# Samples of the cross-attention with the queries as the stationary operand, state space parameters worked out in the input projection, and part of each state space pass on GpSimd

## The chip, the cores and the metric

One core of one Trainium2 chip runs one execution of the kernel. The metric is the device time of that execution in microseconds (us), and it is compared with the time of the kernel before, on the same chip. The engines are named as in the profile: PE is TensorE's matrix multiplication and PEld its weight load, DVE is VectorE, ACT ScalarE, POOL GpSimd, and SP the SyncE queue that issues most transfers.

## What is computed

The reference is one step of a one-layer decoder trunk in float32, for a prompt of 1024 tokens and for 8 samples of 8 tokens each. What matters here:

```python
z = h @ p['w_in']                    # query latent | kv latent | rotary key | state space input
c_q, c_kv, k_r, u = z[..., :256], z[..., 256:512], z[..., 512:544], z[..., 544:]
attn_out = mla_mixer(c_q, c_kv, k_r, pos, p, past)   # samples: 8192 cached positions, paged

# state space: 32 groups of 16 channels, 64 complex states each
dt = jnp.exp(p['ssm_log_dt'])[:, None]
mag = jnp.exp(dt * a_re)
abr, abi = mag * jnp.cos(dt * a_im), mag * jnp.sin(dt * a_im)
bbr, bbi = fr * b_re - fi * b_im, fr * b_im + fi * b_re
# h[t] = a h[t-1] + b u[t], an associative scan over time
y = einsum('blgn,gcn->blgc', hr, c_re) - einsum('blgn,gcn->blgc', hi, c_im) + d * u

# cross-attention, 4 heads of 128, 256 memory tokens
s = jnp.einsum('bqhd,bmhd->bhqm', q, mk) * MEM_SCALE
o = jnp.einsum('bhqm,bmhd->bqhd', softmax(s), mv)
```

The prompt's cross-attention has keys and values of its own, made in this step; each of the 8 samples reads its keys and values (256 tokens, 4 heads) from a cache.

## The kernel before

The work stands in stages, one after the other in the span: the input projection (`stage_in`, to about 131 us), the parallel stage (`stage_par`, 131 to 699), attention over the prompt, the mix, the cross-attention (`stage_mem`, 994 to 1204) and the feed-forward part.

**Input projection.** `stage_in` walks over nine row tiles, t = 8 (the samples) first and then 0 to 7, and multiplies each with the weights of the combined projection (three matmuls per block, since float32 numbers are split into a high and a low half). At t = 2 it calls `dec_start`, which prepares the decode attention and issues its first gathers.

**Parallel stage.** `gen_dec` is the attention of the samples over their cached positions: 16 steps, each with two gathers of latent rows (`kf`) and two of rotary keys (`rf`) that GpSimd issues as indirect DMAs (L1011). `kf` has two buffers, so the gather for step n + 2 waits until step n's value matmuls (`ov`, L1109) have read the buffer. In each step DVE turns the gathered blocks (nine 128x1024 transposes, L1033), PE makes the scores `S` (L1044), DVE takes their maximum `mx` (L1065), ACT the exponentials, PE turns those (`pt`, L1093) and makes `ov`. Beside it run, one after the other, the generators `gen_ssm`, `gen_glu` and others. All instructions of both sides go through the class `Order`, a list scheduler that estimates each instruction's cost and writes the order of PE, DVE, ACT and POOL from that; each engine then runs its list in order.

**State space (`gen_ssm`).** First a parameter part (L617 to L737), some hundred small DVE operations on 128 x 32 to 128 x 256 elements: exponentials as polynomials, angles, powers `pw`, tables `cs8` and `phk` of phases; it loads `prm`, and the samples' inputs `us` in eight scattered loads (L623) that 32 small PE transposes (L736) turn to `Us`. Then eight passes of four groups each. `load(q)` brings `bc` and `h` (L759); `tables(q)` makes W1 (through W1T, transposed on PE at L806), W2 (128 x 576 in three operations, on DVE: two products, `W<-Cst,pw` and `big<-bc,pw`, and their difference `W<-W,big`) and W3, and fills the phase table `csn` by four turns, each doubling its length: two products `big<-csn,phk` and two results `csn<-big,big`. `csn` has one buffer. `chunks(q)` multiplies the inputs with W1, rotates by `csn`, scans (L868), rotates back to `H` and multiplies with W2 and W3. L889 stands for the samples in a chunk, four matmuls a pass, eight in the trace since a float32 matmul is recorded as two. Most elementwise operations go through a helper that the profile shows as L611, so they are told apart by tiles.

**Cross-attention (`stage_mem`).** The prompt goes through in eight tiles; between the tiles stands a list `sample`, pieces of the samples' attention. Before: `sample_k(b)` loads the keys of sample b, 128 x 1024, into a buffer `kv` and makes the scores in eight matmuls (L1777) with a 128 x 128 block of keys stationary and 8 columns of queries moving; `sample_w` and `sample_pT` do the softmax of all samples at once; `sample_v(b)` makes the values the same way (L1809), with a block of values stationary and 8 columns of weights moving. `kv` has two buffers.

## Time and profile before

| | us |
|---|---|
| runs | 2022.9, 2007.9, 2007.51; median 2007.9 |
| profiled execution | 2011.3 |
| its span, first to last instruction | 2009.5 |
| PE busy | 1875.4 (93%) |
| DVE busy | 1099.2 (55%) |
| ACT busy | 802.3 (40%) |
| POOL busy | 515.9 (26%) |

Shares over the whole span hide that stages have different limits, so the windows view cuts the span at the stages' ends: for each stretch its length, the busy time of each engine with its number of instructions, and the granted clock of TensorE as a share of full speed. The views by line give the mean duration of a group of equal instructions; the timeline gives single instructions with their start and duration; the chain of waits follows the work that ended last.

### The profile page before, as it was taken

What the parts mean: (1) busy time and instruction counts of PE and PEld (TensorE: products, weight loads), DVE (VectorE), ACT (ScalarE), POOL (GpSimd) and SP (SyncE); (2) the same over time, 40 slices, a digit from 0 to 9 for tenths busy, and PEclk for the clock granted to TensorE, in tenths of its full rate; (3) what the DMA queues carried; (4) which work ended last, traced back from release to release, by engine and by line L of the source; (5) the groups of instructions that cost most, each with busy time, mean ns of one, the idle gap of its engine ahead of it and who ended that gap; (6) DMA issues with size and microseconds to landing.
All of it is one profiled execution on the core that took longest, in us unless ns stands there. A gap on an engine that the chain in (4) does not pass through costs nothing.

```text
span 2009.5 us, 32068 instructions
## 1 busy us (share of the span) xinstructions
PE 1875.4 (93%) x12747; PEld 1486.4 (74%) x12747; DVE 1099.2 (55%) x2000; ACT 802.3 (40%) x1578; POOL 515.9 (26%) x549
## 2 busy tenths in 40 slices
PE   8967799789898899999999989999999999999997
PEld 6853455355454588777788978888888999999776
DVE  4238999775556588843334464443545533334333
ACT  5312233143332378853333344333444333333332
POOL 1312111131121033325301022222144421110554
PEclk9988889899899999999979999999999999999999
DMA  7713534455477511141123453223333522222221
GB/s 245 234 41 123 198 129 146 143 207 190 156 255 265 151 55 40 64 147 38 66 92 99 148 179 121 93 86 105 94 114 108 170 85 85 81 78 88 74 80 62
DMA packets 136550, 247.94 MB, mean 123 GB/s; under 512 B 26897, under 2 KB 91217, under 8 KB 132305
## 3 DMA queue, kind: packets, MB, share of 16 engines
q1 hardware_dynamic: 129072, 169.87, 27.0%
q0 software_dynamic: 7328, 76.03, 9.9%
q8 instruction: 100, 1.64, 0.3%
q14 instruction: 50, 0.40, 0.1%
HBM read 217.13 MB, written 27.29 MB: 122 GB/s over the span
## 4 chain that ended last, share of the span: by engine, by line
PE 74%; DVE 8%; DMA 6%; issue 5%; ACT 4%; POOL 1%; SPq 1%; DVEq 0%; ACTq 0%; POOLq 0%
PE ps L2069 26%; PE z L1581 5%; PE ps L335 4%; PE ps L337 4%; PE ps L336 4%; PE z L488 4%; PE S L1044 3%; PE ov L1109 3%; DVE kT L1033 2%; PE b L1736 2%; DMA kf<-in_cache_kv_dram,idx 2%; PE t L1384 1%; DMA W<-ky 1%; PE b L335 1%; PE b L336 1%
## 5 line engine op out<-in xcount | busy, mean ns | idle before, releaser
L2069 PE MATMUL ps<-xTl,wh 128*128 128x288 f32 (+1 forms) x1056 | 288.4, 327 | 0.0
L2069 PE MATMUL ps<-xTh,wh 128*128 128x288 f32 (+1 forms) x1056 | 288.2, 327 | 0.0
L2069 PE MATMUL ps<-xTh,wl 128*128 128x288 f32 (+1 forms) x1056 | 288.2, 327 | 0.0
L326 POOL TENSOR_TENSOR wl<-st,wh 128x1024 fp32r<-128x1024 f32 (+1 forms) x52 | 115.8, 2227 | 410.9 <-ACT wh L325 410.9
L1044 PE MATMUL S<-kT,Qb 32*64 32x512 f32 x2304 | 161.6, 663 | 39.2 <-DVE kT L1033 18.0
L326 DVE TENSOR_TENSOR wl<-st,wh 128x1024 fp32r<-128x1024 f32 (+1 forms) x52 | 62.1, 1195 | 246.0 <-ACT wh L325 246.0
L325 ACT ACTIVATE wh<-st 128x1024 fp32r<-128x1024 f32 (+1 forms) x104 | 102.5, 994 | 234.2 <-PE ps L2069 212.5
L2069 PEld LDWEIGHTS ps<-xTh,wh 128*128 128x128 f32 x1056 | 180.1, 189 | 14.1
L2069 PEld LDWEIGHTS ps<-xTl,wh 128*128 128x128 f32 x1056 | 180.0, 189 | 13.8
L2069 PEld LDWEIGHTS ps<-xTh,wl 128*128 128x128 f32 x1056 | 179.9, 189 | 13.9
L326 DVE TENSOR_TENSOR wdl<-std,wdh 128x1024 fp32r<-128x1024 f32 x44 | 100.3, 2282 | 147.3 <-ACT wdh L325 147.3
L1033 DVE STREAM_TRANSPOSE kT<-kf 128x1024 f32<-128x1024 f32 x128 | 151.6, 1220 | 25.2 <-DMA kf<-in_cache_kv_dram,idx 17.5
L2020 POOL TENSOR_TENSOR al<-act,ah 128x1024 fp32r<-128x1024 f32 x44 | 106.8, 2426 | 174.0 <-ACT ah L2019 174.0
L335 PE MATMUL ps<-wdh,ah 128*128 128x512 f32 x352 | 139.5, 396 | 0.0
L336 PE MATMUL ps<-wdl,ah 128*128 128x512 f32 x352 | 139.1, 395 | 0.0
L1109 PE MATMUL ov<-kf,PT 128*64 128x256 f32 x1024 | 128.7, 399 | 0.6 <-ACT PT L1094 0.6
L337 PE MATMUL ps<-wdh,al 128*128 128x512 f32 x352 | 126.1, 396 | 0.0
L1044 PEld LDWEIGHTS S<-kT,Qb 32*64 32x64 f32 x2304 | 44.2, 142 | 98.5 <-issue 41.2
L1109 PEld LDWEIGHTS ov<-kf,PT 128*64 128x64 f32 x1024 | 71.3, 142 | 52.1 <-issue 18.1
L2019 ACT ACTIVATE ah<-act 128x1024 fp32r<-128x1024 f32 (+1 forms) x44 | 49.0, 1113 | 142.2 <-PE ps L336 141.4
L335 PEld LDWEIGHTS ps<-wdh,ah 128*128 128x128 f32 x352 | 66.2, 188 | 17.4 <-issue 0.8
L337 PEld LDWEIGHTS ps<-wdh,al 128*128 128x128 f32 x352 | 66.1, 188 | 15.6
(532 smaller groups left out, 3972.9 us busy)
## 6 DMA issues: line engine op xcount, KB each, us to landing
st<-in_w_gate_dram SPq DMA_DIRECT2D x22, 1024.0 KB
st<-in_w_up_dram SPq DMA_DIRECT2D x22, 1024.0 KB
std<-in_w_down_dram SPq DMA_DIRECT2D x44, 512.0 KB
x<-in_x_prompt_dram SPq DMA_DIRECT2D x16, 512.0 KB
x<-x2d SPq DMA_DIRECT2D x15, 512.0 KB
wst<-in_w_in_dram SPq DMA_DIRECT2D x8, 528.0 KB
xT<-in_xT_dram SPq DMA_DIRECT2D x8, 512.0 KB
ws<-in_w_out_dram SPq DMA_DIRECT2D x8, 512.0 KB
```

What stands on the lines that cost most here:

```text
L325: nc.scalar.activation(hi, src, AF.Copy)
L326: (lo_eng or nc.vector).tensor_sub(lo, src, hi.bitcast(F32))
L335: mm(ps, lh, rh, start=start, stop=False)
L336: mm(ps, lh, rl, start=False, stop=False)
L337: mm(ps, ll, rh, start=False, stop=stop)
L488: nc.tensor.matmul(z[:P, :c1 - c0], lhs[:, k, :P], rhs[:, k, c0:c1], start=a, stop=b)
L1033: V.transpose(t, RF[n] if kb == 8 else KF[n][:, :, :, kb * 32:kb * 32 + 32])
L1044: nc.tensor.matmul(SS[n][half[a], j], Qb[q, kb, 2 * p + a], ts[q, a], start=kb == BLOCKS[0], stop=kb == BLOCKS[-1])
L1109: nc.tensor.matmul(ov[half[a]], PTS[n, g][:, m, half[a]], KF[n][:, a, g * 4 + m], start=g == 0 and m == 0, stop=g == 3 and m == 3)
L1581: nc.tensor.matmul(z[n], l, r[:, n * 512:(n + 1) * 512], start=a, stop=b)
L2020: G.tensor_sub(al, a[:, :, :512], ah[:, :, :512].bitcast(F32))
L2069: nc.tensor.matmul(zt[:, :c1 - c0], l[:, k], r[:, k, c0:c1], start=a, stop=b)
```

## The change

Three edits, which leave what is computed as it was.

1. `gen_ssm` is made in `stage_in` at t = 2 and stepped twice per tile until it yields True; its parameter part so stands among the input projection. The samples' inputs go through a DRAM tile `usd` and back as 32 x 1024, so that 8 transposes take the place of 32. The eight passes stay in `stage_par`.
2. In each pass the three operations of W2 and all operations of the turns go from `nc.vector` (V) to `nc.gpsimd` (G).
3. In the cross-attention the samples' queries are stationary. A pair of samples shares one piece: `sample_s(p)` holds 32 columns of queries (8 real, the rest neighbours or zeros) and moves the 256 columns of a head's keys; the four heads write the four quarters of the partitions. The softmax is made per pair. `sample_v(p)` turns the weights (four transposes), multiplies them stationary with 128 moving columns of values, scales on ACT and turns the result back (two transposes). `kv` has three buffers.

```diff
@@ stage_in
             if t == 2:
-                self.dec_start(lambda: zp.tile([128, 512], F32, tag="z", name="z"))
+                self.dec_start(zbank)
+                self.ssm_groups, opened = self.gen_ssm(zbank), False
+            if 2 < t < 8:
+                for _ in range(2):
+                    opened = opened or next(self.ssm_groups)
+        while not opened:
+            opened = next(self.ssm_groups)
@@ gen_ssm, parameters
-        us8 = new(c2, "us8", [8, 32, 8, 16])
+        usd = self.pool("usd", 1, space=DRAM).tile([8, 32, 8, 16], F32, name="usd")
         for j in range(8):
-            nc.sync.dma_start(us8[:, :, j], self.u_sn.rearrange("(b j) (g c) -> j b g c", j=8, c=16)[j])
+            nc.sync.dma_start(usd[:, :, j], self.u_sn.rearrange("(b j) (g c) -> j b g c", j=8, c=16)[j])
...
+        us = new(c2, "us", [32, 1024], "wide")
+        nc.sync.dma_start(us, usd.rearrange("b (q g) j c -> (b q) (g j c)", q=4))
+        yield
...
-        for g in range(32):
-            nc.tensor.transpose(ps[:, g], us8[:, g].rearrange("p j c -> p (j c)"), self.ident[:8, :8])
+        for g in range(8):
+            nc.tensor.transpose(ps[:, g], us[:, g * 128:(g + 1) * 128], self.ident[:32, :32])
...
+        yield True
@@ gen_ssm, tables(q)
-            tt(V, W2, chb(Cst, 9), pwb(pw[:, 0], 9), OP.mult)
-            yield
-            tt(V, t2, chb(cb, 9), pwb(pw[:, 1], 9), OP.mult)
-            tt(V, W2, W2, t2, OP.subtract)
+            tt(G, W2, chb(Cst, 9), pwb(pw[:, 0], 9), OP.mult)
+            yield
+            tt(G, t2, chb(cb, 9), pwb(pw[:, 1], 9), OP.mult)
+            tt(G, W2, W2, t2, OP.subtract)
...
-                phases(csn, csn[:, :, :, 0:n], phk[:, 0, k - 3, gs], phk[:, 1, k - 3, gs], *(t[:, :, :, 0:n] for t in tq))
+                phases(csn, csn[:, :, :, 0:n], phk[:, 0, k - 3, gs], phk[:, 1, k - 3, gs], *(t[:, :, :, 0:n] for t in tq), e=G)
@@ stage_mem
-        kv = lambda: sp.tile([128, 2, 512], F32, tag="kv", name="kv")
+        kv = lambda: sp.tile([128, 2, 512], F32, tag="kv", name="kv", bufs=3)
...
-        def sample_k(b):
...
-            for k in range(2):
...
-                    nc.tensor.matmul(st[:, k, h, b * 8:(b + 1) * 8], kT[:, h, k], qT[:, h, b * 8:(b + 1) * 8],
-                                     start=True, stop=True)
+        def sample_s(p):
...
+            for j in range(2):
+                b = 2 * p + j
...
+                    nc.tensor.matmul(s[quarter(h), j], smp["qT"][:, h, b * 8:b * 8 + 32], kT[:, h], start=True, stop=True)
...
+            for j in range(2):
+                nc.scalar.activation(Pm[:, j], s[:, j], AF.Exp, bias=mx[:, j:j + 1], scale=MSC, accum_out=l[:, j:j + 1])
...
+        def sample_v(p):
...
+                    nc.tensor.transpose(ps[:, j * 2 + k], Pm[:, j, k * 128:(k + 1) * 128], self.ident)
+            pT = sp.tile([128, 4, 128], F32, tag="pTs", name="pTs", bufs=1)
+            V.tensor_copy(pT, ps)
...
+                        nc.tensor.matmul(po[quarter(h), j], pT[:, j * 2 + k, quarter(h)], vb[:, k, h * 128:(h + 1) * 128],
+                                         start=k == 0, stop=k == 1)
+                nc.scalar.activation(o[:, j], po[:, j], AF.Copy, scale=l[:, j:j + 1])
+            ps = sbank()
+            for j in range(2):
+                nc.tensor.transpose(ps[:, j], o[:, j], self.ident)
...
-            for h in range(4):
-                for k in range(2):
-                    nc.tensor.matmul(po[:, h, b * 8:(b + 1) * 8], vb[:, k, h * 128:(h + 1) * 128],
-                                     pT[:, k, h, b * 8:(b + 1) * 8], start=k == 0, stop=k == 1)
...
-        sample = [[], two(sample_k, 0), two(sample_k, 2), two(sample_k, 4), two(sample_k, 6),
-                  [sample_w, sample_pT] + two(sample_v, 0) + two(sample_v, 2),
-                  two(sample_v, 4) + two(sample_v, 6), [sample_o]]
+        sample = [[], [piece(sample_s, 0)], [piece(sample_v, 0), piece(sample_s, 1)], [piece(sample_v, 1), piece(sample_s, 2)],
+                  [piece(sample_v, 2), piece(sample_s, 3)], [piece(sample_v, 3)], [], [sample_o]]
```

GpSimd's list at the start of the passes, before (in a row: line, operation, the tile written and the tiles read; `x2` marks equal neighbours):

```order
108 L1011 DMA rf<-in_cache_kr_dram,idx 128x512 x2
109 L1011 DMA kf<-in_cache_kv_dram,idx 128x4096 x2
110 L1011 DMA rf<-in_cache_kr_dram,idx 128x512 x2
111 L746 MEMSET W_1615 128x512
112 L746 MEMSET W_1616 128x512
113 L1011 DMA kf<-in_cache_kv_dram,idx 128x4096 x2
```

The same place in the list after (the helper L611 is L619 there, the gathers L1027; `W_1658` is W2 of the first pass):

```order
...
119 L619 TENSOR_TENSOR csn<-big_1644,big_1645 128x4x16 x2
120 L1027 DMA rf<-in_cache_kr_dram,idx 128x512 x2
121 L619 TENSOR_TENSOR big_1644<-csn,phk 128x8x32
122 L619 TENSOR_TENSOR big_1645<-csn,phk 128x8x32
123 L1027 DMA kf<-in_cache_kv_dram,idx 128x4096 x2
124 L619 TENSOR_TENSOR csn<-big_1644,big_1645 128x4x32 x2
125 L619 TENSOR_TENSOR big_1644<-csn,phk 128x512
126 L619 TENSOR_TENSOR big_1645<-csn,phk 128x512
127 L619 TENSOR_TENSOR csn<-big_1644,big_1645 128x4x64 x2
128 L619 TENSOR_TENSOR big_1932<-bc,pw 128x576
129 L619 TENSOR_TENSOR W_1959<-W_1959,big_1932 128x576
130 L1027 DMA rf<-in_cache_kr_dram,idx 128x512 x2
```

The gathers, which stood nearly alone, now stand between the operations of W2 and the turns, in both directions.

SP's list behind the input projection, before (`prm` and `us` are the parameter part's loads, `bc` a pass's):

```order
53 L617 DMA prm<-in_ssm_par_dram 128x128
54 L623 DMA us_1412<-u_sn 8x32x16 x8
55 L514 DMA out_dram<-cn 128x256
56 L515 DMA lat<-cn 128x512
57 L997 DMA msk<-in_k_dmask_dram 128x256
58 L759 DMA bc<-in_ssm_bc_dram 128x256
```

And after:

```order
57 L538 DMA out_dram<-kr_rot 128x256
58 L775 DMA bc<-in_ssm_bc_dram 128x256
59 L776 DMA h_1602<-in_ssm_h_dram 128x64
60 L775 DMA bc<-in_ssm_bc_dram 128x256
61 L776 DMA h_1606<-in_ssm_h_dram 128x64
```

The first loads of the passes stand right behind the projection's last stores; the parameter part's loads stand further ahead, among the projection's own.

PE's list in the cross-attention at the first pair's values, after (`Pms` the samples' weights, `os` their scaled result, the other rows the prompt's):

```order
2547 L1817 MATMUL b<-ident,Pms 128x128 x4
2548 L1827 MATMUL smp<-kv,pTs 32x128 x8
2549 L1863 MATMUL b<-ident,Pm 128x128 x6
2550 L1827 MATMUL smp<-kv,pTs 32x128 x5
2551 L1863 MATMUL b<-ident,Pm 128x128 x2
2552 L1827 MATMUL smp<-kv,pTs 32x128 x3
2553 L1832 MATMUL b<-ident,os 128x128
```

And before, at about the same place (`qTs` the samples' queries, `mv` the prompt's values):

```order
2541 L1709 MATMUL b<-ident,q 128x128 x4
2542 L1777 MATMUL smp<-qTs,kv 128x8 x3
2543 L1850 MATMUL b<-pT,mv 128x128 x7
2544 L1777 MATMUL smp<-qTs,kv 128x8 x13
2545 L1736 MATMUL b<-woh,oh 128x512 x2
```

The matmuls of the samples still stand among the prompt's, and now have transposes ahead of and behind them.

## Rows read from the trace of the kernel before

**Rows 1.** Windows: start:end, length; PE, PEld, DVE, ACT, POOL busy (count); clock, DMA share, GB/s.

```profile
25.00:131.00 106.00, 100.47 (x637) 89.65 (x635) 31.40 (x74) 38.99 (x91) 30.13 (x90) 0.97 0.54 170
131.00:410.00 279.00, 218.84 (x2333) 119.73 (x2333) 252.44 (x564) 77.69 (x213) 46.92 (x54) 0.84 0.42 148
132.00:170.00 38.00, 14.41 (x180) 7.00 (x180) 32.12 (x122) 5.13 (x9) 9.14 (x15) 0.63 0.43 154
245.00:400.00 155.00, 135.40 (x1416) 73.97 (x1424) 142.27 (x284) 46.37 (x130) 23.66 (x23) 0.88 0.37 133
994.00:1204.00 210.00, 200.69 (x1125) 174.56 (x1126) 100.76 (x183) 86.77 (x204) 30.57 (x67) 0.89 0.39 129
1016.00:1026.00 10.00, 10.00 (x40) 8.39 (x39) 1.57 (x5) 1.13 (x5) 0.00 (x0) 0.68 0.17 54
1070.00:1100.00 30.00, 29.17 (x160) 24.64 (x159) 14.93 (x36) 12.14 (x36) 4.13 (x10) 1.00 0.19 70
```

**Rows 2.** Line L889: duration in ns (min/median/max), first and last start, forms.

```profile
L889 PE MATMUL ps<-W,Us x64: 272/273/421, 205.7 to 405.3; 128*8 128x128 f32 x64
```

**Rows 3.** SP's queue: a wait from 131 to 200, and a row of its timeline.

```profile
SPq L759 <- PE ps L736: 43.5, 1, 43.5
181.76 0.33 SPq L759 DMA_DIRECT2D bc<-in_ssm_bc_dram  x1
```

**Rows 4.** The chain of waits from 994 to 1205 us, by line.

```profile
by line: PE b L1736 20.1%; PE b L335 8.4%; PE b L336 8.3%; PE b L337 8.1%; PE smp L1777 7.9%; PE b L1850 7.7%; PE smp L1809 6.5%; PE b L1709 5.6%; issue 4.6%; DMA kv<-in_w_o_dram 3.3%; PE b L1839 2.9%; DVE pt L1744 1.8%; POOL wl L326 1.1%; 
```

**Rows 5.** DVE by line and form, 245 to 400 us: busy us, mean ns of one.

```profile
L1033 DVE STREAM_TRANSPOSE kT<-kf 128x1024 f32<-128x1024 f32 x40 | 48.1, 1224 | 4.0 <-PE S L1044 4.0
L1065 DVE TENSOR_REDUCE mx<-S 128x1 f32<-128x2048 f32 x4 | 9.1, 2283 | 3.5 <-PE S L1044 3.5
L611 DVE TENSOR_TENSOR A<-Z,csn 64x512 f32<-64x512 f32 x10 | 6.9, 693 | 0.2
L611 DVE TENSOR_TENSOR W<-Cst,pw 128x576 f32<-128x576 f32 x5 | 3.7, 742 | 0.0
L611 DVE TENSOR_TENSOR W1T<-W1T,big 128x512 f32<-128x512 f32 x5 | 3.4, 680 | 0.0
L611 DVE TENSOR_TENSOR big<-BB,pw 128x512 f32<-128x512 f32 x5 | 3.4, 675 | 0.0
```

**Rows 6.** Windows, DVE's instructions on the tile big alone.

```profile
245.00:400.00 155.00, 37.38 (x100) 0.88 0.37 133
```

**Rows 7.** POOL by line and form, 130 to 700 us.

```profile
L1011 POOL DMA_INDIRECT rf<-in_cache_kr_dram,idx x30 | 35.8, 1193 | 58.6 <-DVE kT L1033 41.4 <-DVE ky L611 7.9 <-issue 5.3
L1011 POOL DMA_INDIRECT kf<-in_cache_kv_dram,idx x30 | 31.1, 1035 | 156.2 <-PE ov L1109 151.2 <-issue 5.0
L326 POOL TENSOR_TENSOR wl<-st,wh 128x512 fp32r<-128x512 f32 x8 | 10.4, 1297 | 43.6 <-ACT wh L325 43.6
L326 POOL TENSOR_TENSOR al<-attT_s,ah 128x256 fp32r<-128x256 f32 x1 | 0.7, 723 | 61.6 <-ACT ah L325 61.6
L598 POOL TENSOR_TENSOR pt<-pw 128x128 f32<-128x128 f32 x1 | 0.6, 587 | 0.1
```

**Rows 8.** Timelines of DVE and POOL at 427 us: start, duration, instruction.

```profile
427.81 2.32 DVE L1228 SCALAR_TENSOR_TENSOR g<-s,y_s 64x512 f32<-64x512 f32 x1 [1.83 <-ACT s L1226]
427.08 1.27 POOL L1225 TENSOR_TENSOR s<-s,u_all 128x512 f32<-128x512 f32 x1
428.32 1.27 POOL L326 TENSOR_TENSOR wgl<-wg,wgh 128x512 fp32r<-128x512 f32 x1
```

**Rows 9.** DMA issues: count, median us to landing.

```profile
kf<-in_cache_kv_dram,idx POOLq DMA_INDIRECT x32, 11.7
```

**Rows 10.** Timeline of PE, in the cross-attention and in a state space pass.

```profile
261.01 0.40 PE L889 MATMUL ps<-W,Us 128*8 128x128 f32 x8
261.34 1.73 PE L1109 MATMUL ov<-kf,PT 128*64 128x256 f32 x14
1056.17 1.84 PE L1777 MATMUL smp<-qTs,kv 128*128 128x8 f32 x16
```

More of the change, by code (lines that the diff above doesn't have):

```diff
@@ L1180, in side @@
         def side():
[L1181 removed]
+            yield from self.ssm_groups
             yield from self.gen_glu()
@@ L1783, in sample_w @@
+        def sample_v(p):
+            Pm, l = smp.pop(p)
             ps = sbank()
-            s4 = ps.rearrange("p (a k) m -> p a (k m)", a=2)
-            for a in range(2):
+            for j in range(2):
                 for k in range(2):
-                    nc.tensor.transpose(ps[:, a * 2 + k], sT[:, k, 2 * a:2 * a + 2].rearrange("p h t -> p (h t)"),
-                                        self.ident)
-            Pm = smp["P"] = sp.tile([128, 2, 256], F32, tag="Pms", name="Pms", bufs=1)
@@ L1790, in sample_w @@
-            l = sp.tile([128, 4], F32, tag="l8", name="l8")
-            softmax(s4, 2, Pm, l, 0, "mx8")
-        def sample_pT():
-            Pm = smp["P"]
-            ps = sbank()
-            for a in range(2):
-                for k in range(2):
-                    nc.tensor.transpose(ps[:, k * 2 + a], Pm[:, a, k * 128:(k + 1) * 128], self.ident)
-            smp["pT"] = sp.tile([128, 2, 4, 64], F32, tag="sT", name="pTs", bufs=1)
-            V.tensor_copy(smp["pT"].rearrange("p k h t -> p (k h t)"), flat(ps))
-            smp["po"] = ps_.tile([128, 2, 4, 64], F32, tag="smp", name="smp")[:, 0]
@@ L1812, in sample_o @@
+            ps = sbank()
+            for j in range(2):
+                nc.tensor.transpose(ps[:, j], o[:, j], self.ident)
+            V.tensor_copy(smp["oT"].rearrange("p h (b q) -> p b h q", q=8)[:, 2 * p:2 * p + 2],
+                          ps[:, 0:2].rearrange("p b (h q) -> p b h q", q=32)[:, :, :, 0:8])
         def sample_o():
```

70 lines of the change are left out of this document (41 added, 29 removed).

## Prediction

> **What bounds the kernel now.** I read the windows by stage first, since the change touches three stretches with different limits. The profiled execution took 2011.3 us for a span of 2009.5; the median of the runs is 2007.9, so I sum against 2011.3 and take 3.4 off at the end.
>
> In the first part of the parallel stage, from 131 to 410 us, TensorE (PE) is busy 218.84 of 279 us and VectorE (DVE) 252.44 [rows 1]: DVE sets the pace, PE is close behind it. From 132 to 170 us PE is busy 14.41 of 38, while DVE is busy from its start: it works through some hundred small operations of the state space parameters, mixed with decode. The first of the chunks' matmuls L889 stands at 205.7 and the last at 405.3 [rows 2]. With 64 of them in 8 groups of 8 that is 7 cycles in 199.6 us, 28.5 us each. The wait that held the start is in the queue's waits: the table load (L759) stood 43.5 us behind the parameter part's last transposes, L736 [rows 3]. In the steady part, 245 to 400 us, DVE is busy 142.27 of 155 and PE 135.40, at a granted clock of 0.88 [rows 1].
>
> In the cross-attention, 994 to 1204 us, PE is busy 200.69 of 210 [rows 1]: PE bound. The chain there gives 7.9% to L1777 and 6.5% to L1809, the 8-column matmuls of the samples [rows 4].
>
> **Part 1: the parameters move into the input projection.** There DVE is busy 31.40 of 106 us and PE 100.47 [rows 1]. The parameter operations are about 20 us of DVE time: 32.12 busy from 132 to 170 [rows 1] less step 0's nine transposes of 1.224 and a reduction of 2.283 [rows 5] is 18.8, and a few follow. 31.4 + 20 still leaves half of DVE free; PE gets 8 transposes, under 1 us. PE is fed by evictions on DVE and ACT, and a parameter burst ahead of one of these can hold a bank: I take 1 us, range 0 to 4. The queue of loads (SP) gets the 8 scattered stores of `usd` and the reload of `us`; they stand among the loads of `xT`, and their cost is inside that range.
>
> What it gains: without the parameters, step 0's transposes need not wait behind them, and the table load needs no L736. The first pass then needs 205.7 - 181.8 = 24 us [rows 2, 3] from its first table load to its L889, and that load now stands directly behind the projection. With some 10 us for sharing DVE, POOL and PE with step 0, and two tables being made at once, the first L889 should come near 131 + 24 + 10 = 165 us, 40 us earlier.
>
> **Part 2: W2 and the turns go to GpSimd (POOL).** What goes off DVE: all DVE work on the tile `big` in the steady part is 37.38 us [rows 6]; of this the products of W1T and BB stay (3.4 + 3.4), and W<-Cst (3.7) goes as well [rows 5]. That is 34.3 us in 155, or 34.3 x 28.5 / 155 = 6.3 us a pass. DVE's busy time a pass was 142.27 x 28.5 / 155 = 26.2; now 19.9.
>
> What it costs on POOL: no such operation runs there before, so I go by its tensor_tensors of other tiles [rows 7]: 1.297 for 512 columns, 0.723 for 256, 0.587 for 128, and an assumed 0.32 below. One set of turns is 2 x (1.30 + 0.72 + 0.59 + 0.32) + 2 x (0.72 + 0.59 + 0.32 + 0.30) = 9.7 us; W2 of 576 columns is 3 x 1.46 = 4.4. With four gathers of about 1.1 us a step, POOL has 14.1 + 4.5, near 19 us in a pass of 28.5. It fits, if little stands in its way.
>
> What can stand in its way is DVE. At 427.81 a two-input operation of DVE on 64 x 512 took 2.32 us while POOL ran two tensor_tensors from 427.08 to 429.59 [rows 8]; the same width elsewhere takes 0.69 (A<-Z, csn) [rows 5]. It ended half a microsecond after POOL did. The transposes hold 1.224 all along and the reduction 2.283 [rows 5]; both read one tile. So DVE's two-input work, 142.27 - 34.3 - 53.0 for 44 transposes - 9.1 for reductions = 45.9 us, or 8.4 a pass, shares time with POOL's 14.1. The lower bound on the cycle is then 8.4 + 14.1 = 22.5 us (every transpose beside POOL); the upper, 19.9 + 14.1 = 34 (nothing beside POOL, since DVE runs in order and a blocked operation holds the transposes behind it). PE's floor is 135.40 x 28.5 / 155 = 24.9 us a pass at the clock it had. Between 24.9 and 34 I take 29.5, the middle: PE was busy 87% of that stretch with DVE as the bound, it cannot go much above 93%, and some blocking adds to it.
>
> [...]
>
> The order of POOL matters as well: the gathers of `kf` wait for the ov matmuls of a step, 151.2 us in 30 gathers [rows 7], and now W2 and the turns are queued behind such a gather and the gather behind them. A gather delayed by one set of turns comes about 10 us late and takes 11.7 to land [rows 9], 22 of the 28 us that a double buffer gives it; it should show in few steps, by a few microseconds, and I count that into the 29.5.
>
> Sum for the stage: the last chunk output moves from 405.3 to 165 + 7 x 29.5 = 372, a gain of 33 us. As a check from PE: its 217 us of work must then fit between about 140 us (step 0's keys no longer wait) and 372, at 93% busy. That is more than the 87% between 245 and 400 and less than the 96% of the cross-attention [rows 1]; a better clock than 0.88 gives it room. Both orders have the same eight decode steps done at that point and the same rest behind it, so the gain is kept to the stage's end: 31 us with 2 for what collides there. Bounds: cycle 34 gives 165 + 238 = 403, a gain of 2; cycle 27 gives 354, a gain of 51.
>
> **Part 3: the cross-attention's samples.** Removed: 7.9% and 6.5% of the chain's 210 us, 16.6 + 13.7 = 30.3 us [rows 4]. By the timeline 16 of these records take 1.84 us, about 0.11 each although they move 8 columns [rows 10]; 256 x 0.11 = 28 us, the same order. Added: 64 records of 256 columns for the scores. 14 records of that width (L1109) took 1.73 us, 0.124 each [rows 10], giving 7.9; if four quarters run side by side where those ran two, 3.9. For the values 128 records of 128 columns: 8 records of L889, which move 128 too, started at 261.01 and the next line at 261.34, 0.041 each [rows 10], giving 5.3; at most half of 0.124 each, 7.9. Transposes: 24 for 8, 16 more, which I estimate at the 0.11 of the other records, 1.8 us. In all 11 to 17.6 against 30.3: PE saves 13 to 19.
>
> New waits: in every pair the values need pT copied by DVE from the transposes right ahead of them, and the transposes back need ACT's scaling; where the order puts them next to each other PE waits about 1 us. With four pairs and two such places I take 4 us. The clock: it was 0.68 from 1016 to 1026, where a block of L1777 ran, and 1.00 from 1070 to 1100, where few did [rows 1]; at 0.68 ten microseconds do 6.8 of work. Without these blocks some of that comes back; I take 4 of a possible 10. A third `kv` buffer can bring a load forward, 0 to 3. Together 16 - 4 + 4 + 1 = 17, range 4 to 28.
>
> Total: 31 + 17 - 1 = 47 off 2011.3, or 1964; less 3.4, against the median, **1961 us**.
>
> **The rivals.**
> [...] POOL's 14.1 us and DVE do not overlap: cycle 33 to 34 us, stage gain 2 to 9, sum 2007.9 - 5 - 16 = 1987 us. For it: [rows 8], and DVE was 92% busy with the work moved [rows 1]. Against: 13 us of DVE a pass are transposes and reductions, untouched at 1.224 and 2.283 [rows 5].
>
> *POOL becomes the head of the line, slower than before.* The gather of `kf` waits for ov, the turns wait behind it, the chunk waits for the turns' table, and PE waits for the chunk and then holds ov. A cycle of POOL alone is 19 us, plus the waits it already has: 151.2 + 41.4 us in 15 steps of gathers [rows 7], 12.8 a step, makes 32; DVE's blocking on top, up to 8.4, makes 40. Then the last output is at 165 + 280 = 445, 40 later than now, less 16 in the cross-attention: 2032 us. It decides for the worse once the cycle exceeds 28.5 + (40 + 16) / 7 = 36.5 us. Against it: those waits were idle time of an engine with nothing else to do, and turns can fill them.
>
> *The cross-attention gives nothing.* PE's savings are spent in the waits for DVE, ACT and the loads of `kv`, at 994 to 1204; then 2007.9 - 30 = 1978 us. For it: eight new hand-overs, and DMA waits already stand at its start. Against: PE is busy 200.69 of 210 [rows 1], and other chunks' matmuls lie between most of them.
>
> *All of it pays.* PE is the only bound at a clock above 0.95, cycle 27, and the cross-attention keeps a clock of 1.00: 2007.9 - 50 - 26 = 1932 us.
>
> **How the numbers follow.** My forecast (1945 to 1978) has 0.50; the port rival 0.15; the slower rival 0.09; nothing from the cross-attention 0.11; all of it 0.15. The range leaves out about the slower rival and the far end of the best: 1930 to 1996. One per cent, 20 us, is about what a measurement of this kernel can tell from no change. Faster than 1988 are the forecast, the best case, the case without the cross-attention and half of the port rival, less some error of mine in each: 0.78. Within 1%: 0.14, from the other half and misjudged sums. Slower by over 1%: 0.08.
>
> **What would show it.** Right: the first L889 (its number shifts by the added lines) near 165 and the last near 372; DVE busy around 70% between them and PE above 88%; in the cross-attention a span near 193 us, the sample matmuls under 18 us in all, and the granted clock near 1.00 where it was 0.68. The input projection ends at 131 to 135. Wrong: DVE's two-input operations with means of 1 us or more instead of 0.69, waits of DVE or PE on POOL's `csn` or `W`, a cycle above 33 us, or gathers of `kf` that land after their transposes' turn.

## The result, and the profile after

The changed kernel takes 1996.89 us (median of 8 runs, 1989.95 to 2000.77) where the kernel before takes 2013.97 beside it; the ratio is 0.990, 95% interval 0.9876 to 0.9924. That is faster by 1%, 17 us, where 47 were forecast (1961 us). The profiled execution took 1997.27 us for a span of 1995.5, 14.0 less than before.

Where the 14 us come from is read from the first and last start of lines that mark the stages. Before, four lines of matmuls (duration in ns as min/median/max, first and last start in us): the input projection, decode's values, the cross-attention's queries, the feed-forward part.

```profile
L488 PE MATMUL z<-winh,xh x216: 283/288/793, 7.7 to 127.5; 128*128 128x272 f32 x65, 128*128 128x512 f32 x29, 128*64 128x272 f32 x8, 128*64 128x512 f32 x6
L1109 PE MATMUL ov<-kf,PT x1024: 379/379/689, 187.1 to 690.0; 128*64 128x256 f32 x171
L335 PE MATMUL b<-wqh,xh x72: 390/399/775, 996.8 to 1167.7; 128*128 128x512 f32 x64, 128*64 128x512 f32 x8
L2069 PE MATMUL ps<-xTh,wh x1056: 291/297/775, 1203.8 to 1852.4; 128*128 128x288 f32 x117, 128*128 128x512 f32 x59
```

After, the same lines, and L905, which answers to [rows 2]:

```profile
L488 PE MATMUL z<-winh,xh x216: 283/288/793, 8.5 to 141.4; 128*128 128x272 f32 x63, 128*128 128x512 f32 x31, 128*64 128x272 f32 x8, 128*64 128x512 f32 x6
L905 PE MATMUL ps<-W,Us x64: 272/274/421, 178.0 to 406.4; 128*8 128x128 f32 x64
L1125 PE MATMUL ov<-kf,PT x1024: 379/379/690, 186.2 to 696.7; 128*64 128x256 f32 x171
L335 PE MATMUL b<-wqh,xh x72: 388/396/775, 1002.2 to 1145.2; 128*128 128x512 f32 x64, 128*64 128x512 f32 x8
L2092 PE MATMUL ps<-xTh,wh x1056: 291/297/767, 1188.8 to 1838.4; 128*128 128x288 f32 x117, 128*128 128x512 f32 x59
```

| stretch | before | after | difference | forecast |
|---|---|---|---|---|
| start to the projection's last matmul | 127.5 | 141.4 | +13.9 | +1 |
| from there to the last ov | 562.5 | 555.3 | -7.2 | -31 |
| from there to the cross-attention | 306.8 | 305.5 | -1.3 | 0 |
| cross-attention, to the first L2069 (L2092) | 207.0 | 186.6 | -20.4 | -17 |
| rest | 805.7 | 806.7 | +1.0 | 0 |

The cross-attention did what was forecast. The projection lost 14 us that were not, and the parallel stage gained 7 of 31. The first chunk output came at 178.0 and the last at 406.4, where 165 and 372 were forecast: a cycle of (406.4 - 178.0) / 7 = 32.6 us.

The second row of the table can be cut once more, at the first and the last chunk output (L889 before, 205.7 and 405.3; L905 after):

| part | before | forecast | after |
|---|---|---|---|
| projection's last matmul to the first chunk output | 78.2 | 37.5 | 36.6 |
| first to last chunk output, 7 cycles | 199.6 | 207 | 228.4 |
| from there to the last ov | 284.7 | 287 | 290.3 |

The early start came as forecast. Of the 24 us that are missing, 21 lie in the seven cycles.

**The projection.** Waits in the changed kernel between 60 and 145 us (engine and line, what it waited for, sum, times, longest):

```profile
DVE nsgn L627 <- DMA prm<-in_ssm_par_dram: 21.5, 1, 21.5
PE z L488 <- DVE u_all L498: 7.7, 2, 6.3
PE z L981 <- DVE qnT L971: 4.5, 1, 4.5
```

VectorE's first parameter operation waited 21.5 us for `prm`, whose load stands in SP's queue behind the round trip of the queries (`qld`, then `Qb`): it was issued at 83.4 us, and the operation began at 93.9. VectorE ran nothing in between (busy 0.00 us from 72.45 to 93.92): all that stands behind this operation in its list waited as well, and when the load was there the whole burst of parameter operations ran in one go, with the projection's evictions (the operations that read its results `z`) among and behind it. The timelines of PE and DVE show the worst place:

```profile
113.81 0.51 PE L488 MATMUL z<-winh,xh 128*128 128x512 f32 x2
120.64 0.57 PE L488 MATMUL z<-winh,xh 128*128 128x272 f32 x1 [6.32 <-DVE u_all L498]
119.46 0.49 DVE L619 TENSOR_TENSOR cs<-pt,pt 128x128 f32<-128x128 f32 x2
120.03 0.46 DVE L498 TENSOR_SCALAR u_all<-z,rs 128x240 f32<-128x240 f32 x1
```

PE stands from 114.3 to 120.6: the next matmul waits 6.32 us for `u_all`, which reads an earlier `z`, and on VectorE that operation follows the last parameter operations.

**The passes.** DVE by line and form from 200 to 400 us of the changed kernel, answering to [rows 5], and POOL by line and form as in [rows 7]:

```profile
L1049 DVE STREAM_TRANSPOSE kT<-kf 128x1024 f32<-128x1024 f32 x49 | 57.4, 1215 | 6.3 <-PE S L1060 6.3
L619 DVE TENSOR_TENSOR A<-Z,csn 64x512 f32<-64x512 f32 x12 | 8.2, 686 | 0.2
L619 DVE TENSOR_TENSOR W1T<-W1T,big 128x512 f32<-128x512 f32 x6 | 5.2, 874 | 0.2
L619 DVE TENSOR_TENSOR big<-BB,pw 128x512 f32<-128x512 f32 x5 | 5.2, 1040 | 1.3 <-POOL csn L619 1.3
```

```profile
L619 POOL TENSOR_TENSOR big<-csn,phk 128x512 f32<-128x512 f32 x16 | 16.6, 1060 | 0.6
L619 POOL TENSOR_TENSOR csn<-big,big 128x256 f32<-128x256 f32 x16 | 11.5, 741 | 0.5
L619 POOL TENSOR_TENSOR W<-W,big 128x576 f32<-128x576 f32 x8 | 11.6, 1451 | 0.6
L619 POOL TENSOR_TENSOR big<-csn,phk 128x64 f32<-128x64 f32 x16 | 5.9, 384 | 44.7 <-ACT csn L826 34.8 <-DVE BB L619 8.0 <-DVE W1T L619 2.0
```

Transposes are as fast as before (1215 ns against 1224), and of the two-input operations A<-Z is too (686 against 693); others are longer on average, big<-BB 1040 against 675 and W1T<-W1T,big 874 against 680. With the tables back on VectorE (`e1` below) both of these have 680 again in the same window. So the two engines do hold each other up, but in a few operations only: of the five big<-BB three took 0.67 to 0.69 us, two 1.46 and 1.71. Those two, at 292.27 and 357.77, began while GpSimd ran a multiplication of 128 x 576 (291.97 to 293.19 and 357.38 to 358.93); beside one at 327.17, which took 0.69, it was GpSimd's that was longer (1.73 us, where the one at 259.95 took 1.21). Over all forms of VectorE the higher means make 9 us in these 200, some 1.5 a pass (an estimate from the two kernels' means). GpSimd's prices were close or lower: 1060 ns for 512 columns (1297 assumed), 1451 for W2's last (1460 assumed).

**The whole parallel stage.** Windows from the projection's end to the last ov, and two stretches for comparison (columns as in [rows 1]). Changed kernel, then the kernel before:

```profile
142.60:696.70 554.10, 486.69 (x4765) 277.15 (x4766) 374.96 (x574) 180.74 (x447) 190.79 (x255) 0.91 0.48 175
185.00:410.00 225.00, 200.41 (x2062) 107.96 (x2047) 168.71 (x255) 64.72 (x179) 110.68 (x165) 0.91 0.41 152
1002.20:1188.80 186.60, 171.90 (x1071) 137.52 (x1069) 104.52 (x197) 90.19 (x222) 31.18 (x66) 0.95 0.45 148
```

```profile
128.70:690.00 561.30, 477.51 (x4797) 273.19 (x4798) 423.38 (x833) 182.89 (x451) 103.06 (x112) 0.90 0.48 172
996.80:1203.80 207.00, 198.90 (x1118) 172.76 (x1117) 98.39 (x181) 85.85 (x202) 29.56 (x63) 0.90 0.40 130
```

PE is busy 486.7 of 554.1 us, idle 67.4; before it was busy 477.5 of 561.3, idle 83.8. Idle time fell by 16, and the busy time of a stage with as many matmuls less 32 rose by 9. The granted clock stayed at 0.90 to 0.91.

The same view, cut at the first and the last chunk output, shows what filled the cycles. The kernel before, then the changed kernel:

```profile
128.70:205.70 77.00, 44.94 (x510) 22.80 (x513) 65.48 (x188) 18.40 (x47) 16.80 (x30) 0.74 0.33 114
205.70:405.50 199.80, 173.48 (x1826) 96.44 (x1826) 183.54 (x374) 59.19 (x165) 31.45 (x30) 0.89 0.43 154
```

```profile
142.60:178.00 35.40, 20.95 (x229) 11.91 (x232) 27.45 (x40) 5.84 (x17) 24.26 (x37) 0.69 0.50 175
178.00:406.60 228.60, 203.09 (x2075) 109.08 (x2075) 172.28 (x263) 69.60 (x191) 111.92 (x167) 0.90 0.40 145
```

Up to the last chunk output both kernels make the same matmuls but for the 32 transposes removed (2336 and 2304 records, 448 of the 1024 of ov in each). As the passes start earlier, 249 of these records no longer stand ahead of the first chunk but between the chunks. They are decode's: by line there are 1008 records of S for 848 in the second windows, 448 of ov for 384, 112 of pt (L1109, L1093 before) for 92. With them PE's busy time a pass rose from 173.5 / 7 = 24.8 us to 203.1 / 7 = 29.0.

**The cross-attention.** PE by line and form: the samples' scores (L1800), values (L1827) and transposes (L1817, L1832).

```profile
L1827 PE MATMUL smp<-kv,pTs 128*32 128x128 f32 x128 | 5.6, 279 | 0.8 <-DVE pTs L1819 0.8
L1800 PE MATMUL b<-kv,qTs 128*32 128x256 f32 x64 | 4.7, 411 | 0.3 <-DVE oTs L1833 0.3
L1817 PE MATMUL b<-ident,Pms 128*128 128x128 f32 x16 | 2.5, 276 | 0.0
L1832 PE MATMUL b<-ident,os 128*128 128x128 f32 x8 | 2.4, 300 | 0.0
```

10.3 us for scores and values, 4.9 for the transposes; the two lines they replace had 30.3 on the chain [rows 4]. The stage's clock is 0.95 where it was 0.90, PE's busy time 171.9 us where it was 198.9, and its idle time 14.7 where it was 8.1 (windows above).

### The profile page after: what moved, and what is told of

The parts are those of the page before. It is cut to its first block, busy times and chain, and to the rows that moved or that the text cites. A ratio compares the mean times of both kernels' runs of the same rounds, so it can differ in the third digit from the quotient of the medians.

```text
span 1995.5 us, 31989 instructions
## 1 busy us (share of the span) xinstructions
PE 1861.1 (93%) x12675; PEld 1458.1 (73%) x12675; DVE 1072.1 (54%) x1861; ACT 807.7 (40%) x1598; POOL 610.5 (31%) x702
## 4 chain that ended last, share of the span: by engine, by line
PE 61%; ACT 3%; issue 3%; DVE 3%; DMA 2%; POOL 1%; SPq 0%; DVEq 0%; ACTq 0%; POOLq 0%
PE ps L2092 26%; PE z L1597 5%; PE ps L335 4%; PE ps L337 4%; PE ps L336 4%; PE b L1752 2%; DMA kf<-in_cache_kv_dram,idx 1%; PE t L1400 1%; PE S L1060 1%; PE ov L1125 1%; PE o L1417 1%; PE o L1416 1%; PE s L1378 1%; PE b L1874 1%; PE b L335 1%
## 5 line engine op out<-in xcount | busy, mean ns | idle before, releaser
L2092 PE MATMUL ps<-xTh,wh 128*128 128x288 f32 (+1 forms) x1056 | 288.7, 328 | 2.4 <-DVE pt L1487 2.4
L2092 PE MATMUL ps<-xTl,wh 128*128 128x288 f32 (+1 forms) x1056 | 288.7, 328 | 0.0
L2092 PE MATMUL ps<-xTh,wl 128*128 128x288 f32 (+1 forms) x1056 | 288.6, 328 | 0.0
L2092 PEld LDWEIGHTS ps<-xTh,wh 128*128 128x128 f32 x1056 | 180.3, 189 | 16.9 <-issue 2.8
L2092 PEld LDWEIGHTS ps<-xTh,wl 128*128 128x128 f32 x1056 | 180.1, 189 | 14.1
L2092 PEld LDWEIGHTS ps<-xTl,wh 128*128 128x128 f32 x1056 | 180.3, 189 | 13.9
L1060 PEld LDWEIGHTS S<-kT,Qb 32*64 32x64 f32 x2304 | 45.6, 136 | 66.6 <-issue 41.9
```

The costliest lines, as they stand in the source:

```text
L1060: nc.tensor.matmul(SS[n][half[a], j], Qb[q, kb, 2 * p + a], ts[q, a], start=kb == BLOCKS[0], stop=kb == BLOCKS[-1])
L2092: nc.tensor.matmul(zt[:, :c1 - c0], l[:, k], r[:, k, c0:c1], start=a, stop=b)
```

## The experiments

All times are medians beside runs of the kernel before; the difference is told against the kernel named. There are five sets of runs (e1 to e4, e5 to e8, e9 to e12, e13 to e15, e16 to e18), and the kernel before has a median between 2008.9 and 2013.9 us in them (2014.0 beside the changed kernel), so a difference between two sets is uncertain by some 5 us (an estimate from these medians). The ratios are to the kernel before in the same set.

### One part at a time

Edits: `e1` puts W2 and the turns back on VectorE (`tt(G, W2, ...)` to `tt(V, W2, ...)`, `e=G` left out); `e2`, `e3`, `e4` are the kernel before with one part of the diff each.

> The changed kernel with W2 and the turns back on VectorE; the early parameters and the new cross-attention stay. My theory: in the stretch 185 to 410 us PE is the limit (busy 89% at a granted clock of 0.91), and work taken from VectorE there is off the path, so this run is within 8 us of the changed kernel (ratio to before 0.985 to 0.996), the projection still ends near 141 us, and the last chunk matmul stands between 400 and 415. [...] Second rival: VectorE would bound again, 15 us or more slower than the changed kernel.

> The kernel before with only W2 and the turns on GpSimd. My theory: PE is close behind VectorE in that stretch, so 0 to 8 us faster than before, with VectorE busy under 80% between 250 and 350 us where it was 99%. Rival (GpSimd holds the pass): 5 to 20 us slower than before, with cycles of 30 us or more. Rival (VectorE was the only bound): 20 us or more faster.

> The kernel before with only the new cross-attention. The milestones of the two traces give 20 us for that stage; I expect 17 to 23 us faster than before, thus at least as fast as the whole change. Rival: part of the stage's gain comes from the shift of what stands before it; then under 12 us.

> The kernel before with only the early parameters (tables on VectorE, old cross-attention). My theory: the projection ends 12 to 16 us later, since VectorE's burst of parameter operations stands ahead of the evictions, and the parallel stage gives back 5 to 14: total 0 to 10 us slower than before. Rival: the late end is caused by GpSimd's work too, or by chance; then the projection ends within 5 us of before and the kernel is 5 to 15 us faster.

| run | us | ratio to before, interval | projection's last matmul | last chunk output | last ov |
|---|---|---|---|---|---|
| changed kernel | 1996.9 | 0.990 (0.9876 to 0.9924) | 141.4 | 406.4 | 696.7 |
| e1, without GpSimd | 1983.9 | 0.9851 (0.9825 to 0.9877) | 140.0 | 403.1 | 690.8 |
| e2, GpSimd alone | 2011.9 | 0.9988 (0.9966 to 1.0009) | 127.1 | 406.9 | 690.7 |
| e3, cross-attention alone | 1992.7 | 0.9903 (0.9878 to 0.9928) | 126.8 | 407.4 | 690.6 |
| e4, parameters alone | 2012.1 | 0.9992 (0.9969 to 1.0014) | 140.2 | 400.4 | 687.4 |

The cross-attention alone gives the whole of the gain. The early parameters give nothing alone: they end the projection 13 us late and win that back by the end of decode. GpSimd alone gives nothing, and in the changed kernel 13 us less than nothing (10 by the ratios). e3 and e4 came out as expected. e1's time lies in the 10 to 25 us that were expected if GpSimd's tables hold each pass, its last chunk output in the 400 to 415 of its theory, so it does not decide between them. In e2 VectorE was still busy 84.92 us of the 100 from 250 to 350, where under 80% was expected.

### The late load, and what sets the pace

```diff
# e5, on e1
+        self.prm = pers.tile([128, 4, 32], F32, name="prm")
+        nc.sync.dma_start(self.prm, i["ssm_par"])
...
-        prm = new(c2, "prm", [128, 4, 32])
-        nc.sync.dma_start(prm, i["ssm_par"])
+        prm = self.prm
# e6, on e1: the chunk's first product four times
-            for g in range(NG):
+            for g in [g for g in range(NG) for _ in range(4)]:
                 nc.tensor.matmul(pa[:, g], W1[:, g], U[:, g], start=True, stop=True)
# e7, on e1: each turn twice
+                for _ in range(2):
                     phases(csn, ...)
# e8, on the changed kernel: turns in the first pass only
+                if q:
+                    return
                 phases(csn, ...)
```

> The version with tables on VectorE, early parameters and new cross-attention, and in addition the parameters' load at the start of the projection instead of behind the query's round trip. My theory: VectorE stood 21.5 us waiting for that load and then held the evictions of two tiles; without it the projection ends at 128 to 134 us instead of 140, and the kernel is 5 to 12 us faster than the same without the early load. Rival: the burst itself delays the evictions wherever it stands; then the projection still ends after 137 us and the time is the same within 4 us. Further rival: an earlier end of the projection is lost again by the end of the decode steps.

> The version with tables on VectorE, early parameters and new cross-attention; in each state space pass the chunk's first product is made four times instead of once (the same result written again). That is 3 x 8 records a pass more for TensorE, at 0.15 us each some 3.5 us a pass and 28 us in all. My theory, TensorE bounds that part: 18 to 30 us slower. Rival, another engine's chain sets the pace: under 10 us slower.

> The version with tables on VectorE, early parameters and new cross-attention; VectorE makes each turn of the phase table twice (the same values), 4.3 us a pass and 34 us in all. My theory: VectorE is not the limit, so under 10 us slower. Rival, VectorE sets the pace (as its 99% busy time in the kernel before suggests): 25 us or more slower.

> The changed kernel with the turns on GpSimd made in the first pass only; the other seven passes leave them out and use the first pass's phases. It takes about 9 us a pass off GpSimd. [...]

e5: 1973.0 us (0.9807, 0.9771 to 0.9842), 11 less than e1. Its projection and PE's waits there:

```profile
L490 PE MATMUL z<-winh,xh x216: 283/288/793, 8.2 to 132.0; 128*128 128x272 f32 x63, 128*128 128x512 f32 x31, 128*64 128x272 f32 x8, 128*64 128x512 f32 x6
PE z L982 <- DVE qnT L972: 2.8, 1, 2.8
PE ps L789 <- DVE u_all L500: 0.7, 1, 0.7
```

The projection ends at 132.0, and the waits of the projection's matmuls for `u_all` are gone (the 0.7 left is the first pass's own). The other versions agree, whatever their tables, their order and their other edits: with the early load (e5, e11 to e15, e18) the projection ends between 129.9 and 132.6, with the late one (the changed kernel and nine others) between 138.0 and 142.4. This settles the projection: the late load cost some 8 to 9 us of the 13.9, and the early parameters as such the other 4.5 (132.0 against 127.5).

e6: 1986.2 (0.9889), 2 us more than e1 (8 by the ratios). e7: 2010.6 (0.9996), 27 more. e8, which leaves out seven of the eight sets of turns: 1976.6 (0.9814), 20 less than the changed kernel (17 by the ratios). e6 and e7 came out against their theories and as their rivals, and e8 above the 8 to 15 that were expected if GpSimd's tables cost the changed kernel its loss. Taken alone, e6 says that TensorE does not bound, e7 that VectorE does, and e8 that the turns on GpSimd cost the changed kernel 20 us. Yet even without the turns e8's cycle is (391.2 - 175.4) / 7 = 30.8 us, above the 29.5 of the forecast, with PE busy 190.3 us in it, 27.2 a pass.

### One buffer or two for the phase table

After a pass the turns wait for ACT's first entries, and these for the last reader of `csn` (a serial loop, since `csn` has one buffer). The changed kernel's wait of POOL from 185 to 410 us:

```profile
POOL big L619 <- ACT csn L826: 34.8, 5, 12.6
```

```diff
# e9, on the changed kernel; e11 on e5; e12 on the changed kernel with e5's load
-        csn = new(sp, "csn", [128, 2, NG, 128])
...
+            csn = two("csn", q, [128, 2, NG, 128])
+            TB[q] = h0, U, W1, W2, csn
# e10, on e1
+            for _ in range(6):
+                tt(V, spare[1], spare[0], spare[0], OP.mult)
```

> The changed kernel with two buffers for the phase table csn instead of one. Theory A, the turns on GpSimd stand in a serial loop (ACT's first entries wait for the chunk's last reader of csn, then some 9 us of turns, then the next chunk): the cycle falls by 3 us or more and the kernel is 12 to 25 us faster than the changed kernel. [...] Theory C, the decode steps alone set the pace: within 3 us.

> The version with tables on VectorE, early parameters and new cross-attention, plus six operations of 128 x 512 a pass on VectorE into a spare tile that nothing reads: 6 x 0.68 = 4.1 us a pass, 33 us in all, as much as the second turns, but in no chain. If VectorE's capacity sets the pace, 20 to 30 us slower, as the second turns were (27). If the second turns cost by lengthening the serial loop through csn, under 12 us slower.

> The version with tables on VectorE, early parameters, early load and new cross-attention, with two buffers for csn. If the serial loop costs on VectorE too: 5 us or more faster than the same with one buffer (1973). If VectorE's capacity bounds: the same within 4 us.

> The changed kernel with the early load and two buffers for csn. If the loop through csn was what GpSimd's tables cost and VectorE's capacity bounds otherwise, this is the fastest of all: 1950 to 1968 us. [...]

e9: 1980.3 (0.9843, 0.9799 to 0.9887), 17 less than the changed kernel (12 by the ratios), and the wait for `csn` on POOL is gone. e10: 2003.3 (0.9954), 19 more than e1 for 33 us of work. e11: 1975.4 (0.9811), the same as e5 within the scatter. e12: 1965.9 (0.9769, 0.9733 to 0.9806), faster than both kernels. In time all four lie at or near what the serial loop through `csn` and VectorE's load would give. But e9's cycle fell by 1.8 us only, to (392.8 - 176.9) / 7 = 30.8, where its theory A wanted 3 or more, and e10's 19 lie just under the 20 to 30 expected.

### The best version loaded

> The version with tables on GpSimd, two buffers for csn, early load and new cross-attention (1966), with the chunk's first product made four times, 3.5 us of TensorE a pass by the earlier estimate. If TensorE has taken over as the limit there, 12 to 28 us slower; if not, under 6 us slower, as on the version with tables on VectorE (2).

> The same version (1966) with six spare operations of 128 x 512 a pass on VectorE, 4.1 us a pass. [...]

> The same version (1966) with W2 back on VectorE and the turns alone on GpSimd: 2.2 us a pass more on VectorE, 4.2 less on GpSimd. [...]

e13 (e6's edit on e12): 2011.1, 45 us more than e12 for an estimated 28 us of work (192 records at the 0.145 us of the same product in the kernel before: 56 records in 8.1 us from 200 to 410). e14 (six spare operations as in e10, on one tile that they read and write): 2002.1, 36 more for 33. e15 (W2 back on VectorE): 1988.7, 23 more where 2.2 us a pass moved. All three lie beyond every range expected (for e13 12 to 28 if TensorE is the limit; 15 to 28 for e14 and 5 to 12 for e15 if VectorE sets the pace). One engine's load does not explain them together, and the same TensorE work cost 2 us on e1. PE's busy time in the parallel stage rose by 37.3 us from e12 to e13 (468.2 to 505.5), at a granted clock of 0.93 and 0.91, and by 13.7 from e1 to e6 (472.4 to 486.0), at 0.91 and 0.94, for the same added matmuls. In e13 the last chunk output stands at 409.7 and the last ov at 716.7: 307 us for the second half, where e12 has nearly the same work (2569 matmul records for 2619) in 668.4 - 381.9 = 286.5. Something that every edit touches cost time in stretches that the edit left alone.

### The order alone

One thing that every edit touches is the list that the class `Order` writes. It prices every instruction; each edit gives it other starts, and it writes other lists for the whole stage. So the last three runs change the price of a TensorE instruction and nothing else:

```diff
# in Order.cost, e16 on the changed kernel, e17 on e1, e18 on e12
-            return 1.1 * t, 1.1 * t + 250.0
+            return 1.05 * t, 1.05 * t + 250.0
```

> The changed kernel with the list scheduler's price of a TensorE instruction at 1.05 instead of 1.1 times its estimate: the same work in a somewhat other order. If orders of equal work differ by little, within 5 us of the changed kernel (1997). If the order alone decides 10 us or more, the difference between GpSimd and VectorE for the tables (13) is no more than an order's luck.

> The version with tables on VectorE, early parameters and new cross-attention, with the same other price. If the 13 us by which tables on VectorE beat GpSimd (1984 to 1997) are the work's, the two stand 8 to 18 us apart here too; if they are the order's, they move closer than 5 us or change places.

> The version with tables on GpSimd, two buffers for csn, early load and new cross-attention (1966), with the same other price. If its lead of some 31 us over the changed kernel is the buffer's and the load's, it stays 20 to 40 us ahead of the changed kernel with this price; if it is an order's luck, it falls back to 1980 or more.

| version | price 1.1 | price 1.05 | last ov, 1.1 and 1.05 |
|---|---|---|---|
| changed kernel (GpSimd) | 1996.9 | 1969.3 (0.9788, 0.9741 to 0.9835) | 696.7, 660.7 |
| tables on VectorE | 1983.9 | 1989.8 (0.9884, 0.9839 to 0.9929) | 690.8, 685.0 |
| GpSimd, two buffers, early load | 1965.9 | 1966.9 (0.977, 0.9726 to 0.9815) | 668.4, 661.0 |

The changed kernel's own work, in another order, takes 28 us less (23 by the ratios). GpSimd for the tables, which lost 13 us to VectorE at the one price, wins 20 at the other: e16 and e17 changed places, as expected if the 13 were the order's. The two other versions moved by 6 and 1 us only. And the two buffers with the early load, worth 31 us at the one price, are worth 2 at the other, although the projection does end 8 us earlier (129.9 against 138.0). e18 met neither of its expectations: it stayed fast, and e16 caught up with it. So what the loop through `csn` costs depends on the order that was written: theory A of e9 does not hold in general.

The window of the parallel stage in e16, and that between its first and last chunk output:

```profile
139.20:660.70 521.50, 461.41 (x4767) 261.02 (x4766) 373.85 (x574) 180.03 (x447) 192.78 (x255) 0.94 0.52 187
170.70:387.00 216.30, 189.60 (x2079) 103.91 (x2079) 176.28 (x268) 70.80 (x198) 112.36 (x166) 0.92 0.45 165
```

Against the changed kernel (above): 521.5 us for 554.1 in the profiled executions. The matmuls are the same, 4767 records to 4765, and PE's idle time is 60.1 to 67.4. The busy time is 461.4 to 486.7: 25 of the 33 us are the same matmuls taking longer. Two things are seen in it. The granted clock of the stage is 0.91 in the changed kernel and 0.94 in e16; if matmuls take longer as the clock is lower (80 scores of the kernel before, from 371.95 to 379.06 at 0.63, have a mean of 875 ns, the 80 of e16 below at 1.00 one of 592), some 16 of the 25 us go with it (an estimate: 486.7 x 0.91 = 443 and 461.4 x 0.94 = 434 leave 9). Whether the order brought the clock about no run shows. And the weight loads of the scores wait for nothing that the profile shows ("issue") longer, 41.9 us to 33.3 (waits of PEld, sum, times, longest; the changed kernel, then e16). This sum does not follow the times of the versions in general: it is 41.2 in the kernel before and 34.6 in e7, which takes as long.

```profile
PEld S L1060 <- issue: 41.9, 154, 0.8
```

```profile
PEld S L1060 <- issue: 33.3, 130, 0.6
```

One place shows such waits within a busy PE. The scores S in the changed kernel, 56 records in 6.92 us, and in e16, 80 records in 4.55:

```profile
265.43 6.92 PE L1060 MATMUL S<-kT,Qb 32*64 32x512 f32 x56
268.34 0.13 PEld L1060 LDWEIGHTS S<-kT,Qb 32*64 32x64 f32 x1 [0.53 <-issue]
269.03 0.20 PEld L1060 LDWEIGHTS S<-kT,Qb 32*64 32x64 f32 x4 [0.57 <-issue]
269.76 0.14 PEld L1060 LDWEIGHTS S<-kT,Qb 32*64 32x64 f32 x2 [0.52 <-issue]
```

```profile
247.14 4.55 PE L1060 MATMUL S<-kT,Qb 32*64 32x512 f32 x80
```

Both stretches have a granted clock of 1.00, and a single matmul takes 587 ns in either. In the changed kernel the loads come in small groups with 0.5 to 0.7 us of "issue" between them; in one such microsecond the DMA engines are busy 0.93, in another 1.12, in e16's stretch 0.19 (the first two rows count PE and PEld on this line alone):

```profile
268.10:269.10 1.00, 0.93 (x8) 0.20 (x4) 1.00 0.93 393
271.10:272.10 1.00, 1.00 (x15) 0.26 (x11) 1.00 1.12 477
```

```profile
247.20:251.60 4.40, 4.40 (x82) 1.60 (x80) 3.32 (x5) 1.07 (x4) 1.33 (x2) 1.00 0.19 45
```

## Why the prediction was wrong, point by point

- *The parameters cost the projection 1 us (0 to 4).* Wrong: 13.9. Half of VectorE was free as said, but the burst ran late, from 93.9 to 119.9, among the evictions. The step that failed is the queue of loads: the prediction named the stores of `usd` and the reload of `us`, put their cost "inside that range", and left out the load of `prm`. The diff puts this load behind `dec_start`, whose store and reload of the queries hold SP (8.8 us for `qld` alone), and VectorE's later work stood with its first operation, 21.5 us. With the load at the start the projection ends at 132.0 (e5), 4.5 us later than before, which is still just beyond the 0 to 4.
- *The first chunk near 165, the last near 372, cycle 29.5.* The start of 178.0 is the forecast plus the late projection (165 + 13.9 = 179), so the mechanism of the early start was right. The step that failed is the cycle: "I take 29.5, the middle" between 24.9 and 34, with 32.6 measured. The term that was mis-sized is PE's floor of "24.9 us a pass", taken from the steady part of the old kernel. There a good part of decode's matmuls ran ahead of the first chunk; as the passes start earlier, 249 records of them fall between the chunks, and PE's busy time a pass is 29.0 us (27.1 in e16's order, 27.2 in e8 without the turns). With 29.0 PE would have had to be busy 98% of a cycle of 29.5. GpSimd's work was 8.6 + 4.1 us a pass against 9.7 + 4.4 reckoned, the operations that GpSimd made longer cost VectorE little (some 1.5 us a pass, the estimate above), and the gathers waited less (kf 89.1 us for ov, 151.2 before), so these prices were not what failed. The wait for `csn` cost something in this order: the other order (e16), two buffers (e9) and no turns (e8) each take the cycle to 30.8 or 30.9. But no version with the early parameters has a cycle under 30.5 us (e12) or PE busy more than 90% of it. What was not reckoned either is the order: the sum took a new list for granted as good as the old. With e16's list the cycle is (386.7 - 170.7) / 7 = 30.9 and the whole stage 522.7 us (660.7 - 138.0) from the projection's last matmul to the last ov, 39.8 less than before. So the stage's gain of 31 was to be had, though by a shorter time behind the chunks (274.0 us) and not by the cycle of the forecast.
- *PE would be 93% busy, a better clock giving it room.* Between the first and the last chunk output PE was busy 89% (203.1 of 228.6 us) at a clock of 0.90, and VectorE 75%. The check spread 217 us of work evenly from 140 to 372. Ahead of the first chunk PE is busy 21.0 of 35.4 us only, so with this some 196 us were left for the 207 between the chunks, 95%, more than the 93% that the check allowed.
- *The cross-attention, -17.* Right in its mechanism, and the total near: -20.4, and -19 alone (e3). The matmuls took 10.3 us (9.2 to 15.8 reckoned). The terms were larger than reckoned, and in part made up for each other: PE's busy time fell by 27.0 us, where 16 + 4 were taken for matmuls and clock, and its idle time rose by 6.6, where 4 were taken for waits. The stage's clock rose as said, from 0.90 to 0.95, but part of that can be scatter: e4, whose samples are the old ones, has 0.93 in this stage and 200.6 us. One reading was not exact: the block of L1777 stands at 1013.3 to 1016.6, right ahead of the stretch at a clock of 0.68 (1016 to 1026), in which the prompt's matmuls ran.
- *The base.* The 3.4 us between the profiled execution and the median came from three runs; with eight the median of the kernel before is 2014.0, above the profiled 2011.3. The gain is not touched by this.
- *The rivals.* The first (the "port rival" of the chances: POOL's 14.1 us and DVE without overlap, 1987 us) came nearest in time but not by its mechanism: A<-Z stayed at 686 ns, what GpSimd made longer is some 1.5 us of VectorE a pass (the estimate above), and in e16, 28 us faster, the operations that do suffer are longer still in the same window (big<-BB 1212 ns, W1T<-W1T,big 1051). That operations of VectorE are longer beside GpSimd is seen in big<-BB, 1040 ns against 675, and not in A<-Z, 686 against 693; what makes them longer no run shows. How much the order alone can take back is shown by e16. That GpSimd becomes the head of the line did not come: the cycle stayed under 36.5. Nor did a cross-attention without gain, or the case that all of it pays (cycle 27).
- *Stays open.* What GpSimd is worth for the tables when the order is left out of it: -20 and +13 us are both measured. By the same scatter e6, e7, e8, e10 and e13 to e15 do not decide between TensorE and VectorE as the stage's limit. What in the order makes the same matmuls take longer, clock or late issue, and which of these comes first, is open too. And 1973 to 1966, e5 to e12, is less than an order's scatter.

The fastest are e12 (1965.9), e18 (1966.9) and e16 (1969.3), 2.1 to 2.3% under the kernel before.

## What to carry to other kernels

Where a list scheduler writes the order, measure the unchanged work under two or three of its prices first: the spread (28, 6 and 1 us for the three versions here) is the size below which a part of a change, or an experiment that undoes a part, can hardly be read. When work is moved ahead, follow its loads through the queue they are put in, and ask what else the engine that waits for them holds back (VectorE stood 21.5 us here, with all that was behind). When a stage starts earlier, count again what else then runs beside it: a floor per pass that was read from the old trace holds for the old mixture. Matmuls with 8 moving columns were worth turning round here, so that the operand with many columns moves: 33.8 us of busy time on L1777 and L1809 became 10.3, with transposes of 4.9.

## What the runs showed of the hardware that was not expected

The same records of the parallel stage were 486.7 us of PE's busy time in one order and 461.4 in another. PE's own issue was late in a stretch that counts as busy: 56 matmuls took 6.92 us at a clock of 1.00 while `kf` and `rf` were being gathered and the DMA engines were busy 0.93 and 1.12 in the two microseconds shown, where others go at 0.057 us each. What the issue waited for no row shows, and other stretches at a high DMA share ran at full pace (80 records in 4.55 us from 645.85, at a share of 1.01), so contention is a suspicion here, not a finding. The same added matmuls cost PE 13.7 us of busy time in one version (e6) and 37.3 in another (e13), the granted clock having gone from 0.91 to 0.94 in the one and from 0.93 to 0.91 in the other. GpSimd's two-input multiplication of 128 x 512 took 1060 ns with a broadcast factor, less than the 1297 of [rows 7].
